# Merging two masked key blocks into one row with a predicated copy, in a hybrid decoder layer

## Chip, core and metric

The kernel runs on one core of a Trainium2 chip. The metric is device time in microseconds (us). A core has five engines that the profile names PE (TensorE, matrix multiply, with PEld for its weight loads), DVE (VectorE), ACT (ScalarE), POOL (GpSimd) and SP (SyncE, which here issues every DMA). Each runs its own queue of instructions in order and waits on semaphores for what other engines produce.

## What is computed

One decoder layer over 1024 tokens, width 1024: an input projection feeds three groups of heads (sliding-window attention, a gated linear recurrence, and a chunked delta-rule state update), and an output projection, a residual sum and a LayerNorm end it. The change is in the attention:

```
qb = q.reshape(bsz, nb, BLOCK, A_KV_HEADS, grp, HEAD_DIM) * (HEAD_DIM ** -0.5)
kb, vb = band(k), band(v)                      # previous block of 128 keys and own block: 256 keys
s = einsum("bnqhgd,bnkhd->bnhgqk", qb, kb)
diff = qi + BLOCK - kj
band_mask = (diff >= 0) & (diff < WINDOW)      # BLOCK = WINDOW = 128
s = where(mask, s, -inf)
m = maximum(max(s, axis=-1), sink)
p = exp(s - m)
denom = sum(p, axis=-1) + exp(sink - m)
o = einsum("bnhgqk,bnkhd->bnqhgd", p / denom, vb)
```

Query i of a block may see key j of the previous block only if j > i, and key j of its own block only if j <= i. So each of the 128 positions j belongs to exactly one of the two blocks, and each query sees exactly 128 keys (in the first block of the sequence only those of its own block).

## The kernel before

The sequence is worked in two halves (h = 0, 1) of 512 tokens. Every projection is a set of matmuls with 512 columns, three for each product of 128 rows, because weights and inputs are split into a high and a low part (`wh_`/`wl_`, `xh`/`xl`). Their results stand in PSUM tiles `pj_...` (`pj_q0` to `pj_q3` the queries of two heads each, `pj_ak` and `pj_av` the keys and values, `pj_ga`, `pj_gb`, `pj_gc` the gates, `pj_k`, `pj_r`, `pj_v` the state group's inputs). ACT makes the high parts of the weights, POOL or DVE the low ones, by two lists of names. PSUM has eight banks in three rings: three for `pj`, two for the state group (`rw`), three (`g`) that the attention's `sp`, `tp`, `pv` share with the recurrence's `lg`.

Attention has 32 blocks, named h_g_n: half, pair of heads, block of 128 queries. `evac_q` copies a projected query tile out of PSUM (ACT the high part, DVE the low one). `scores_stream` then runs for each block: four matmuls into `sp` (2 heads x 256 keys); on DVE one custom reduction for each head that masks, scales, writes the negated scores to SBUF `s` and leaves the row's bound in `mn`; on ACT an exponential of 257 columns for each head (the sink is column 256, put there by POOL) that also sums the row; a reciprocal on DVE; on POOL the sum of the two halves of 128 columns; and on DVE one scaling for each head. `turn_stream` transposes the row on PE into `tp`; DVE multiplies it by a triangle `pmask` for the previous block's part of `PT`, ACT or DVE copies `tp`, and POOL subtracts to get the own block's part. `pv_stream` multiplies `PT` by the values. Four of the 32 blocks (n = 0 of h = 0) have no previous block, and take 128 columns.

Around it run the state group and the recurrence. The state group's scores `sc` lead over DRAM to a triangular inverse, which DVE does in 31 steps of two instructions for each half (`it`, `TW`, after a first product `G`). `rwkv_v` puts centred values into `UV` (row sums `ms` of the transposed `vp`). `rwkv_chain` then goes through eight chunks in order for each half: PE `ch`, a copy `u0`, PE `ch` again, copies into `UV`, PE again, and the new state `S` (two DVE instructions) that is copied into `UV` for the next chunk. The output projection `o` comes last, and its first half fills PE between chunks of the second half.

What sets the order: the generators (`scores_stream`, `rwkv_stream` and so on) are merged by a string of letters (`MERGED`), which fixes the program. Then a table `ISSUED` puts every engine's instructions into another order, as numbers that index that engine's own list; dependencies between neighbours of the new order are added without a semaphore. The table comes from a planner that is not in the file. Nearly all instructions carry the line 248 in the profile, that of the helper which records them (237 in the changed kernel), so they are told apart by tiles.

Of the kernel before, what the change touches and what calls it, by code (L numbers as in the profile page):

```python
# [1338 lines left out]
```

## Time and profile before

| | before |
|---|---|
| median of 3 runs | 524.44 us |
| lowest and highest run | 524.26 and 528.27 us |
| the profiled execution, its own time | 519.97 us |
| its span in the profile | 518.2 us |
| mean granted TensorE clock | 0.985 |
| PEld, DVE, ACT, POOL busy | 365.0, 381.0, 258.1, 240.1 us |
| DMA moved | 46.30 MB, mean 89 GB/s |

The profiled execution ran 4.5 us below the median of the three runs; its span and the 1.8 us around it make up its own 519.97 us. Busy time of an engine is the union of its instructions. For PE that is nearly the whole span, so what is to be read is where PE sits idle or runs at a lower clock, who ends those waits, and what that engine had in its queue ahead of the awaited instruction. The rows follow in the prediction.

### The profile page before, as it was taken

To read this page: it belongs to the slowest core of one execution; us is meant where nothing else is said; L and a number is where in the kernel's file an instruction comes from. 1 tells how busy PE (TensorE), PEld (TensorE's weight loads), DVE (VectorE), ACT (ScalarE), POOL (GpSimd) and SP (SyncE) were. 2 spreads that over 40 slices of the span, in tenths; PEclk is the share of its full clock that TensorE was granted. 3 is DMA by queue.
4 is the path that set the end of the run, shared out by engine and by line. 5 is a ranking of instruction groups with operands and counts; after the bars stand their busy time and mean duration, and the time that the engine had idled before them with its cause. 6 is when DMAs were issued, how large, how long until landed. Compare 5 with 4: busy or idle time off the path is not lost.

```text
span 518.2 us, 8768 instructions
## 1 busy us (share of the span) xinstructions
PE 485.7 (94%) x3086; PEld 365.0 (70%) x3086; DVE 381.0 (74%) x916; ACT 258.1 (50%) x535; POOL 240.1 (46%) x285
## 2 busy tenths in 40 slices
PE   8999989979989899999998979999899899999994
PEld 6777667756766667677676858866666567878884
DVE  5966797898995478668658888888967523649984
ACT  4327737554646737475777434448746436400000
POOL 4621564144657202332567625666777606644010
PEclk9999999989999999999999999999999899999998
DMA  8900214221214432322131522311171017013531
GB/s 279 337 0 1 63 42 100 84 82 41 63 40 88 127 103 63 122 62 86 59 101 42 123 81 67 97 46 56 62 130 46 24 39 244 0 41 123 202 133 71
DMA packets 45979, 46.30 MB, mean 89 GB/s; under 512 B 25832, under 2 KB 27112, under 8 KB 45936
## 3 DMA queue, kind: packets, MB, share of 16 engines
q1 hardware_dynamic: 45936, 45.75, 29.0%
q8 instruction: 24, 0.39, 0.3%
q14 instruction: 19, 0.16, 0.1%
HBM read 39.95 MB, written 5.78 MB: 88 GB/s over the span
## 4 chain that ended last, share of the span: by engine, by line
PE 61%; DVE 23%; DMA 5%; issue 3%; ACT 3%; SPq 2%; POOL 2%; DVEq 0%; ACTq 0%; POOLq 0%
PE o L248 17%; PE c L248 5%; PE pj_ga L248 4%; DVE s L248 3%; PE pj_q L248 3%; PE ch L248 3%; PE pj_xb L248 3%; PE pj_r L248 2%; PE sp L248 2%; PE pj_gc L248 2%; SPq L248 2%; PE pj_k L248 2%; PE yp L248 2%; PE pv L248 2%; DVE TW L248 2%
## 5 line engine op out<-in xcount | busy, mean ns | idle before, releaser
L248 ACT ACTIVATE s<-s,mn 128x257 f32<-128x257 f32 (+1 forms) x64 | 31.4, 492 | 21.2 <-DVE mn L248 19.2
L248 PE MATMUL o<-wol,yh 128*128 128x512 f32 (+1 forms) x90 | 32.9, 370 | 0.0
L248 PE MATMUL o<-woh,yh 128*128 128x512 f32 (+1 forms) x90 | 32.5, 377 | 0.0
L248 PE MATMUL o<-woh,yl 128*128 128x512 f32 (+1 forms) x90 | 32.4, 373 | 0.0
L248 PE MATMUL o<-wo,yh 128*128 128x512 f32 (+1 forms) x108 | 32.1, 372 | 0.0
L248 POOL TENSOR_TENSOR s<-s 128x256 f32<-128x256 f32 x28 | 21.3, 765 | 22.6 <-ACT s L248 13.8
L248 DVE CUSTOM_DVE_ANT_0 s<-sp,con,dv 128x256 f32<-128x256 f32 (+1 forms) x64 | 27.2, 461 | 4.7 <-PE sp L248 4.4
L248 PE MATMUL pj_ga<-xh,wl_ga 128*128 128x512 f32 x64 | 26.5, 415 | 2.3 <-DVE wl_ga L248 2.3
L248 POOL TENSOR_TENSOR wl_ga<-wr_ga,wh_ga 128x512 fp32r<-128x512 f32 x14 | 19.1, 1365 | 20.2 <-ACT wh_ga L248 17.7
L248 DVE TENSOR_SCALAR s<-s,mn 128x128 f32<-128x128 f32 x64 | 26.0, 428 | 2.7 <-POOL s L248 2.7
L248 PE MATMUL pj_ga<-xh,wh_ga 128*128 128x512 f32 x64 | 26.3, 413 | 0.0
L248 PE MATMUL pj_ga<-xl,wh_ga 128*128 128x512 f32 x64 | 26.0, 406 | 0.0
L248 PE MATMUL pj_q<-xl,wh_q 128*128 128x512 f32 x64 | 25.8, 403 | 0.0
L248 POOL TENSOR_TENSOR PT<-PT 128x256 f32<-128x256 f32 x28 | 21.0, 755 | 10.3 <-ACT PT L248 9.4
L248 PE MATMUL pj_q<-xh,wh_q 128*128 128x512 f32 x64 | 25.7, 402 | 0.0
L248 PE MATMUL pj_q<-xh,wl_q 128*128 128x512 f32 x64 | 25.5, 401 | 0.0
L248 POOL TENSOR_TENSOR mv<-mv,ec 128x1 f32<-128x1 f32 x8 | 5.9, 737 | 41.7 <-DVE mv L248 41.7
L248 DVE TENSOR_TENSOR TW<-TW,it 128x126 f32<-128x126 f32 (+22 forms) x62 | 23.6, 381 | 0.8
L248 POOL TENSOR_TENSOR yl<-y,yh 128x512 fp32r<-128x512 f32 x16 | 22.0, 1393 | 3.5 <-PE o L248 1.9
L248 DVE SCALAR_TENSOR_TENSOR xres<-xres,mv,ln 128x512 f32<-128x512 f32 x32 | 23.5, 775 | 0.1
L248 PE MATMUL sp<-KH,q 128*128 128x256 f32 (+1 forms) x64 | 18.6, 314 | 5.0 <-DVE q L248 3.9
L248 PE MATMUL pv<-PT,vtok 128*64 128x128 f32 x240 | 21.4, 288 | 1.1 <-DVE PT L248 1.1
(347 smaller groups left out, 1546.1 us busy)
## 6 DMA issues: line engine op xcount, KB each, us to landing
xr<-in_xT SPq DMA_DIRECT2D x16, 256.0 KB, 3.6
wr_ga<-in_w_t SPq DMA_DIRECT2D x16, 256.0 KB, 2.6
wr_q<-in_w_t SPq DMA_DIRECT2D x16, 256.0 KB, 2.5
wor<-in_w_o SPq DMA_DIRECT2D x16, 256.0 KB, 3.1
xres<-in_x SPq DMA_DIRECT2D x8, 512.0 KB, 3.2
out<-xres SPq DMA_DIRECT2D x16, 256.0 KB, 2.0
wr_xb<-in_w_t SPq DMA_DIRECT2D x8, 256.0 KB, 2.7
wr_gb<-in_w_t SPq DMA_DIRECT2D x8, 256.0 KB, 2.6
```

Source lines behind the costliest of these rows:

```text
L248: self.ins.append(getattr(self.engine, op)(*args, **kw).ins)
```

## The change

The scale 1/8 moves from the reduction into `evac_q`. The scores stay in PSUM: a predicated copy on DVE writes the previous block's scores over the own block's columns where j > i (in the first block a constant of -1e30), so that one row of 128 remains. Column 127 of the previous part, which is no longer needed, takes the sink. A reduction over 129 columns gives the negated maximum of both heads at once, and the exponential reads those 129 columns of PSUM and writes `s`. The two halves need no sum any more. The scaling by the reciprocal moves from DVE to ACT. After the transpose, one DVE product with both triangles (`pmask` is now 256 wide) writes both parts of `PT`.

```
 def evac_q(g, h, ps):
-            A.copy(q[rs, j], ps[rs])
+            A.activation(q[rs, j], ps[rs], AF.Copy, scale=0.125)
-            V.tensor_sub(q[HS[1 - j], j], ps[rs], q[rs, j].bitcast(F32))
+            V.scalar_tensor_tensor(q[HS[1 - j], j], ps[rs], 0.125, q[rs, j].bitcast(F32),
+                                   op0=ALU.mult, op1=ALU.subtract)
...
 def scores_stream():
-                    st = wt("s", (128, 2, 257), NS, name=f"s_{h}_{g}_{n}")
+                    st = wt("s", (128, 2, 129), NS, name=f"s_{h}_{g}_{n}")
...
+                    past = neg.unsqueeze(2).broadcast_to([128, 2, 128]) if w0 else sp[:, :, 0:128]
+                    V.copy_predicated(sp[:, :, 128:256], prevm, past)
+                    V.tensor_copy(sp[:, :, 127:128], PR["sink"][:, g::4].unsqueeze(2))
+                    V.tensor_reduce(mn[:, 0:2], sp[:, :, 127:256], axis=AX.X, op=ALU.max, negate=True)
                     for j in range(2):
-                        hq = g + 4 * j
-                        P.tensor_copy(st[:, j, 256:257], nsink[:, hq:hq + 1])
-                        V.tensor_tensor_reduce(st[:, j, w0:256], sp[:, j, w0:256], C["amask"][:, w0:256],
-                                               scale=-0.125, scalar=nsink[:, hq:hq + 1], op0=ALU.add,
-                                               op1=ALU.min, accum_out=mn[:, j:j + 1])
-                        A.activation(st[:, j, w0:257], st[:, j, w0:257], AF.Exp, scale=-1.0,
-                                     bias=mn[:, j:j + 1], accum_out=mn[:, 2 + j:3 + j])
+                        A.activation(st[:, j], sp[:, j, 127:256], AF.Exp, bias=mn[:, j:j + 1],
+                                     accum_out=mn[:, 2 + j:3 + j])
                     V.reciprocal(mn[:, 2:4], mn[:, 2:4])
-                        (V if CE[n % len(CE)] else P).tensor_add(st[:, :, 128:256], st[:, :, 128:256],
-                                                                 st[:, :, 0:128])
                     for j in range(2):
-                        V.tensor_scalar_mul(st[:, j, 128:256], st[:, j, 128:256], mn[:, 2 + j:3 + j])
+                        A.activation(st[:, j, 1:129], st[:, j, 1:129], AF.Copy, scale=mn[:, 2 + j:3 + j])
...
 def turn_stream():
-                V.tensor_mul(PT[:, 0], tp, C["pmask"].unsqueeze(1).broadcast_to([128, 2, 128]))
-                    copy(f"pt{h}{g}{n}", PT[:, 1], tp)
-                    P.tensor_sub(PT[:, 1], PT[:, 1], PT[:, 0])
+                V.tensor_mul(PT, tp.unsqueeze(1).broadcast_to([128, 2, 2, 128]),
+                             C["pmask"].rearrange("p (b t) -> p b t", b=2).unsqueeze(2)
+                             .broadcast_to([128, 2, 2, 128]))
...
 ISSUED = {
 "vector": (
-    "82 84 83 80-81 48-49 0-2 5 4 3 6-8 10 9 41 38-39 50 46 51 42 40 37 76 43-44 36 45 35 47 162 52 34 53-54 56 "
...
```

PE keeps its 2461 instructions and SP its 196. DVE goes from 918 to 815, ACT from 473 to 516, POOL from 290 to 170. All five orders in `ISSUED` are new; `MERGED` and the two lists of who splits and copies what are as before. Three places matter below. A name such as `wl_ga2_0_0` is the low part of one half of the weights of gate tile ga2 in the first half of the sequence.

First, DVE in the first half of the sequence, around the split `wl_ga2` and the query split `q0`. Before, in the middle of the inverse:

```order
L248 TENSOR_TENSOR it_0_5_834<-G_0_708,TW_0_711 128x78
L248 SCALAR_TENSOR_TENSOR y_0_4_965<-tr_0_0_949,G_gb0_0_923 128x512
L248 TENSOR_TENSOR TW_0_711<-TW_0_711,it_0_5_834 128x26x3
L248 COPY hlast_461<-tr_0_0_949 128x1
L248 TENSOR_TENSOR it_0_6_855<-G_0_708,TW_0_711 128x100
L248 COPY xb_1_0_1067<-xbc_460 128x3
L248 TENSOR_TENSOR TW_0_711<-TW_0_711,it_0_6_855 128x25x4
L248 COPY xbc_460<-xb_1_0_1067 128x3
L248 TENSOR_TENSOR it_0_7_858<-G_0_708,TW_0_711 128x96
L248 TENSOR_TENSOR wl_ga2_0_0_1151<-wr_ga2_0_0_1071,wh_ga2_0_0_1150 128x512
L248 TENSOR_TENSOR TW_0_711<-TW_0_711,it_0_7_858 128x24x4
```

The same engine and place in the changed kernel, ahead of the inverse's first step:

```order
L237 TENSOR_REDUCE ms_0_0_763<-vp_0_0_758 128x8
L237 TENSOR_TENSOR wl_ga2_0_0_1151<-wr_ga2_0_0_1071,wh_ga2_0_0_1150 128x512
L237 SCALAR_TENSOR_TENSOR UV_0_757<-ms_0_0_763,vp_0_0_758 64x4x64
L237 TENSOR_REDUCE ms_0_1_774<-vp_0_1_769 128x8
L237 SCALAR_TENSOR_TENSOR UV_0_757<-ms_0_0_763,vp_0_0_758 64x4x64 x3
L237 SCALAR_TENSOR_TENSOR UV_0_757<-ms_0_1_774,vp_0_1_769 64x4x64 x4
L237 SCALAR_TENSOR_TENSOR q0_0_1172<-pj_q0_0_1129,q0_0_1172 64x512
L237 TENSOR_TENSOR G_0_708<-G_0_708,dd_0_534 128x1024
L237 SCALAR_TENSOR_TENSOR q0_0_1172<-pj_q0_0_1129,q0_0_1172 64x512
L237 SCALAR_TENSOR_TENSOR G_ga0_0_1120<-G_ga0_0_1120,pj_ga0_0_1077 128x512
L237 TENSOR_TENSOR it_0_0_716<-G_0_708,TW_0_711 128x31
```

The split `wl_ga2` stood behind seven steps of the inverse and half of the eighth, and now stands ahead of all of them; the query split stands around the product `G`, where it used to follow the ninth step.

Second, PE in the second half, at the first scores `sp_1_0_0`. Before:

```order
L248 MATMUL vp_1_0_3057<-con_63,xs_v0_1_2801 128x128 x4
L248 MATMUL pj_gb1_1_3389<-xh_1_1_2343,wl_gb1_1_0_3306 128x512
L248 MATMUL pj_gb1_1_3389<-xh_1_2_2354,wh_gb1_1_0_3305 128x512
L248 MATMUL vp_1_1_3068<-con_63,xs_v1_1_2842 128x128 x2
L248 MATMUL pj_gb1_1_3389<-xl_1_2_2355,wh_gb1_1_0_3305 128x512
L248 MATMUL pj_gb1_1_3389<-xh_1_2_2354,wl_gb1_1_0_3306 128x512
L248 MATMUL pj_xb1_1_3577<-xh_1_0_2339,wh_xb1_1_0_3546 128x512
L248 MATMUL sp_1_0_0_3340<-KH_465,q0_1_3321 128x256
```

In the changed kernel:

```order
L237 MATMUL pj_q0_1_3232<-xh_1_7_2394,wl_q0_1_1_3223 128x512
L237 MATMUL pj_ga1_1_3676<-xh_1_0_2287,wl_ga1_1_0_3617 128x512
L237 MATMUL pj_ga1_1_3676<-xh_1_1_2291,wh_ga1_1_0_3616 128x512
L237 MATMUL pj_ga1_1_3676<-xl_1_1_2292,wh_ga1_1_0_3616 128x512
L237 MATMUL pj_ga1_1_3676<-xh_1_1_2291,wl_ga1_1_0_3617 128x512
L237 MATMUL pj_ga1_1_3676<-xh_1_2_2302,wh_ga1_1_0_3616 128x512
L237 MATMUL pj_ga1_1_3676<-xl_1_2_2303,wh_ga1_1_0_3616 128x512
L237 MATMUL pj_ga1_1_3676<-xh_1_2_2302,wl_ga1_1_0_3617 128x512
L237 MATMUL pj_ga1_1_3676<-xh_1_3_2327,wh_ga1_1_0_3616 128x512
L237 MATMUL pj_ga1_1_3676<-xl_1_3_2328,wh_ga1_1_0_3616 128x512
L237 MATMUL sp_1_0_0_3288<-KH_465,q0_1_3269 128x256
```

The scores moved behind the projections xb1, ga0 and part of ga1: between the last `sc` of the half and `sp_1_0_0` the PE queue held 48 matmuls of 512 columns, and now holds 91. On DVE the split of `q0_1`, which these scores wait for, stood behind six steps of the inverse and now stands behind nine.

Third, DVE in the chain of the second half, from the state of chunk 1 to its copy into `UV`. Before:

```order
L248 TENSOR_TENSOR PT_1_3_2_4430<-tp_1_3_2_4427,con_63 128x256
L248 TENSOR_TENSOR S_1_1_4120<-ch_1_1_3963,S_1_0_3938 128x128
L248 TENSOR_TENSOR S_1_1_4120<-S_1_1_4120,wc_1_2557 128x128
L248 TENSOR_SCALAR s_1_3_3_4232<-s_1_3_3_4232,mn_1_3_3_4233 128x128
L248 COPY UV_1_3056<-S_1_1_4120 64x2x64
```

In the changed kernel:

```order
L237 TENSOR_TENSOR PT_1_2_3_4004<-tp_1_2_3_4001,con_63 128x512
L237 TENSOR_TENSOR S_1_1_4020<-ch_1_1_3879,S_1_0_3854 128x128
L237 TENSOR_REDUCE mn_1_3_0_4075<-sp_1_3_0_4076 128x2
L237 TENSOR_TENSOR S_1_1_4020<-S_1_1_4020,wc_1_2505 128x128
L237 COPY UV_1_3004<-S_1_1_4020 64x2x64
L237 COPY_PREDICATED sp_1_3_1_4091<-con_63,sp_1_3_1_4091 128x2x128
L237 COPY sp_1_3_1_4091<-par_64 128x2
```

The scaling of a late attention block that stood between the state and its copy is gone from this engine; a reduction of an earlier block stands between the two instructions of the state instead. On PE the last matmul of `sp_1_3_3`, the last scores of all, stood inside chunk 0 of this chain and now stands behind chunk 3.

More of the change, by code (lines that the diff above doesn't have):

```diff
@@ L48 @@
 X0 = (1, 0, 0, 0, 0, 0, 0, 0)
-CE = (0,)
-ME = (0,)
 OL = (0,)
@@ L220 @@
 for _name, _w in (("ident", 128),
-                  ("smask", 128), ("amask", 256), ("pmask", 128)):
+                  ("smask", 128), ("prev", 128), ("pmask", 256)):
     CON[_name] = slice(_n, _n + _w)
@@ L400, in hybrid_kernel @@
     fs, fb = (dcol(2), dcol(2)), (dcol(2), dcol(2))
-    bab, nsink = dcol(4), dcol(8)
+    bab, neg = dcol(4), dcol(1)
     sp4, nsp4 = dcol(2), dcol(2)
@@ L413, in hybrid_kernel @@
     V.tensor_scalar_mul(bab, PR["bab"], 0.5)
-    V.tensor_scalar_mul(nsink, PR["sink"], -1.0)
+    V.memset(neg, NEG)
     sc = s(pers, "sc", [128, 16], 1)
@@ L920, in evac_q @@
         for j, rs in enumerate(HS):
-            A.copy(q[rs, j], ps[rs])
+            A.activation(q[rs, j], ps[rs], AF.Copy, scale=0.125)
         for j, rs in enumerate(HS):
-            V.tensor_sub(q[HS[1 - j], j], ps[rs], q[rs, j].bitcast(F32))
+            V.scalar_tensor_tensor(q[HS[1 - j], j], ps[rs], 0.125, q[rs, j].bitcast(F32),
+                                   op0=ALU.mult, op1=ALU.subtract)
         Q[g] = q
     PV, AQ, BQ = {}, [], []
+    prevm = C["prev"].bitcast(mybir.dt.uint32).unsqueeze(1).broadcast_to([128, 2, 128])
     def scores_stream():
@@ L942, in scores_stream @@
                         TE.matmul(sp[:, j, w0:256], q[:, j, qs], KL[:, j, ks], start=False, stop=True)
+                    past = neg.unsqueeze(2).broadcast_to([128, 2, 128]) if w0 else sp[:, :, 0:128]
+                    V.copy_predicated(sp[:, :, 128:256], prevm, past)
+                    V.tensor_copy(sp[:, :, 127:128], PR["sink"][:, g::4].unsqueeze(2))
+                    V.tensor_reduce(mn[:, 0:2], sp[:, :, 127:256], axis=AX.X, op=ALU.max, negate=True)
                     for j in range(2):
-                        hq = g + 4 * j
-                        P.tensor_copy(st[:, j, 256:257], nsink[:, hq:hq + 1])
-                        V.tensor_tensor_reduce(st[:, j, w0:256], sp[:, j, w0:256], C["amask"][:, w0:256],
-                                               scale=-0.125, scalar=nsink[:, hq:hq + 1], op0=ALU.add,
-                                               op1=ALU.min, accum_out=mn[:, j:j + 1])
-                        A.activation(st[:, j, w0:257], st[:, j, w0:257], AF.Exp, scale=-1.0,
-                                     bias=mn[:, j:j + 1], accum_out=mn[:, 2 + j:3 + j])
+                        A.activation(st[:, j], sp[:, j, 127:256], AF.Exp, bias=mn[:, j:j + 1],
+                                     accum_out=mn[:, 2 + j:3 + j])
                     V.reciprocal(mn[:, 2:4], mn[:, 2:4])
-                    if not w0:
-                        (V if CE[n % len(CE)] else P).tensor_add(st[:, :, 128:256], st[:, :, 128:256],
-                                                                 st[:, :, 0:128])
                     for j in range(2):
-                        V.tensor_scalar_mul(st[:, j, 128:256], st[:, j, 128:256], mn[:, 2 + j:3 + j])
+                        A.activation(st[:, j, 1:129], st[:, j, 1:129], AF.Copy, scale=mn[:, 2 + j:3 + j])
                     AQ.append((h, g, n, st, w0 // 128))
@@ L968, in turn_stream @@
             for j in range(2):
-                TE.transpose(tp[:, j], st[:, j, 128:256], ident)
+                TE.transpose(tp[:, j], st[:, j, 1:129], ident)
             PT = wt("PT", (128, 2, 2, 128), 4, name=f"PT_{h}_{g}_{n}")
@@ L973, in turn_stream @@
             else:
-                V.tensor_mul(PT[:, 0], tp, C["pmask"].unsqueeze(1).broadcast_to([128, 2, 128]))
-                if ME[n % len(ME)]:
-                    V.tensor_sub(PT[:, 1], tp, PT[:, 0])
-                else:
-                    copy(f"pt{h}{g}{n}", PT[:, 1], tp)
-                    P.tensor_sub(PT[:, 1], PT[:, 1], PT[:, 0])
+                V.tensor_mul(PT, tp.unsqueeze(1).broadcast_to([128, 2, 2, 128]),
+                             C["pmask"].rearrange("p (b t) -> p b t", b=2).unsqueeze(2)
+                             .broadcast_to([128, 2, 2, 128]))
             BQ.append((h, g, n, PT, b0))
@@ L1278, in _constants @@
     c["smask"] = np.concatenate([sI < t, sI <= t], 1).astype(f)
-    diff = i[:, None] + 128 - np.arange(256)[None, :]
-    c["amask"] = np.where((diff >= 0) & (diff < 128), 0.0, NEG).astype(f)
-    c["pmask"] = (i[:, None] > i[None, :]).astype(f)
+    c["prev"] = (i[:, None] < i[None, :]).astype(f)
+    c["pmask"] = np.concatenate([i[:, None] > i[None, :], i[:, None] <= i[None, :]], 1).astype(f)
     return c
```

220 rows, old and new, of the table ISSUED are left out of this document.

## The prediction

> **What bounds the kernel now.** I read the page's busy times first, then the span cut into stages, then what PE waited for, then narrow windows behind the longest waits, and last the groups of the instructions that the change touches.
>
> ```profile
> span 518.2 us, 8768 instructions
> ...
> PE 485.7 (94%) x3086; PEld 365.0 (70%) x3086; DVE 381.0 (74%) x916; ACT 258.1 (50%) x535; POOL 240.1 (46%) x285
> ...
> 100.00:160.00 60.00, 54.56 (x291) 39.64 (x290) 54.65 (x180) 32.86 (x87) 30.73 (x50) 0.97 0.19 58
> 300.00:400.00 100.00, 92.05 (x648) 68.21 (x646) 84.58 (x238) 57.26 (x137) 62.18 (x83) 0.98 0.27 72
> 60.00:100.00 40.00, 37.34 (x204) 28.59 (x203) 33.09 (x63) 21.78 (x36) 20.70 (x21) 1.00 0.25 67
> 160.00:300.00 140.00, 135.40 (x1001) 99.88 (x1001) 95.65 (x191) 89.97 (x167) 60.16 (x63) 1.00 0.33 91
> 400.00:430.00 30.00, 27.95 (x319) 19.30 (x318) 12.13 (x31) 12.30 (x36) 10.86 (x10) 0.94 0.14 46
> ```
>
> The columns after a window and its length are the busy time of PE, PEld, DVE, ACT and POOL, then the clock. PE is the bound, and the change takes no matmul away. So at most PE's idle time can go, and what a lower clock costs. Between 60 and 430 us PE idles 5.4 + 8.0 + 2.7 + 4.6 + 2.1 = 22.8 us. In the two stretches with attention (100 to 160, 300 to 400) DVE is 91% and 85% busy, so DVE sets the pace there wherever PE waits:
>
> ```profile
> PE sp L248 <- DVE q L248: 3.9, 2, 3.2
> PE tp L248 <- DVE s L248: 1.7, 4, 0.7
> PE tp L248 <- DVE mn L248: 1.4, 1, 1.4
> PE pv L248 <- DVE PT L248: 1.1, 1, 1.1
> ...
> 106.30 0.50 PE L248 MATMUL pj_ga<-xh,wl_ga 128*128 128x512 f32 x1 [2.31 <-DVE wl_ga L248]
> 307.75 0.50 PE L248 MATMUL sp<-KH,q 128*128 128x256 f32 x2 [3.23 <-DVE q L248]
> 405.80 0.45 PE L248 MATMUL ch<-UV,X 128*64 128x64 f32 x6 [1.82 <-DVE UV L248]
> ...
> 107.20:110.60 3.40, 3.23 (x8) 1.99 (x6) 3.37 (x4) 1.60 (x3) 2.81 (x2) 0.54 0.55 154
> 308.60:312.00 3.40, 3.40 (x13) 2.88 (x13) 3.15 (x10) 0.62 (x1) 0.00 (x0) 0.54 0.00 0
> 407.60:411.00 3.40, 3.40 (x25) 2.31 (x24) 1.23 (x4) 1.90 (x6) 1.41 (x2) 0.54 0.00 0
> ```
>
> The first rows are sums of waits (total, times, longest), the next ones the three longest waits where they ended, and the last ones windows again. The three are for `wl_ga` (2.3 us, up to 106.3), `q` (3.2, up to 307.75) and `UV` (1.8, up to 405.8). A little behind each lies a stretch of 3.4 us in which the clock was 0.54, so that it lost 0.46 x 3.4 = 1.6 us of matmul work.
>
> **The change on each engine.** These groups carry the prices:
>
> ```profile
> L248 DVE CUSTOM_DVE_ANT_0 s<-sp,con,dv 128x256 f32<-128x256 f32 (+1 forms) x64 | 27.2, 461 | 4.7 <-PE sp L248 4.4 <-PE tp L248 0.2
> L248 DVE TENSOR_SCALAR s<-s,mn 128x128 f32<-128x128 f32 x64 | 26.0, 428 | 2.7 <-POOL s L248 2.7
> L248 DVE DVE_READ_ACCUMULATOR2_ANT mn<- 128x1 f32 x64 | 5.2, 81 | 0.0
> L248 DVE TENSOR_TENSOR PT<-tp,con 128x256 f32<-128x256 f32 x28 | 11.6, 420 | 3.9 <-PE tp L248 3.5
> L248 DVE TENSOR_TENSOR X<-sc,con 128x256 f32<-128x256 f32 x16 | 6.3, 414 | 1.5 <-PE sc L248 1.3
> L248 DVE RECIPROCAL mn<-mn 128x2 f32<-128x2 f32 x32 | 5.0, 160 | 4.9 <-ACT s L248 4.5
> L248 DVE TENSOR_REDUCE ms<-vp 128x8 f32<-128x512 f32 x4 | 2.6, 682 | 0.0
> L248 DVE TENSOR_TENSOR y<-bo,xs_v 128x512 f32<-128x512 f32 x4 | 2.7, 684 | 0.8 <-PE bo L248 0.8
> L248 DVE TENSOR_TENSOR q<-pj_q,q 64x512 fp32r<-64x512 f32 x16 | 11.0, 688 | 4.0 <-ACT q L248 3.7
> ...
> L248 ACT ACTIVATE s<-s,mn 128x257 f32<-128x257 f32 (+1 forms) x64 | 31.4, 492 | 21.2 <-DVE mn L248 19.2 <-POOL PT L248 1.4
> L248 ACT ACTIVATE s<-s,mn 128x129 f32<-128x129 f32 x8 | 3.2, 401 | 4.1 <-DVE mn L248 4.1
> L248 ACT COPY UV<-S 64x128 f32<-64x128 f32 x15 | 4.5, 299 | 6.3 <-DVE S L248 6.2
> L248 ACT COPY PT<-tp 128x256 f32<-128x256 f32 x24 | 8.9, 371 | 19.3 <-DVE PT L248 19.1
> L248 ACT CAST q<-pj_q 64x512 fp32r<-64x512 f32 x16 | 9.2, 578 | 3.2 <-PE pj_q L248 3.0
> ...
> L248 POOL TENSOR_TENSOR s<-s 128x256 f32<-128x256 f32 x28 | 21.3, 765 | 22.6 <-ACT s L248 13.8 <-DVE s L248 6.4 <-PE pj_q L248 1.6
> L248 POOL TENSOR_TENSOR PT<-PT 128x256 f32<-128x256 f32 x28 | 21.0, 755 | 10.3 <-ACT PT L248 9.4 <-DVE PT L248 0.7
> L248 POOL COPY s<-dv 128x1 f32<-128x1 f32 x64 | 12.7, 234 | 17.3 <-PE tp L248 12.0 <-DVE TW L248 1.7 <-issue 1.3
> ```
>
> DVE loses 27.2 + 26.0 + 5.2 + 11.6 = 70.0 us. It gets 32 predicated copies of 256 elements, which the trace doesn't show. The nearest row is the masked product `X` out of PSUM with 256 elements, 0.414 us; I take that. The upper bound is 0.684, the `y` row with 512 elements, if the copy passes twice over its data; the lower bound 0.34, half of the `ms` reduction. The 32 sink copies of two elements go by the reciprocal's 0.16 (5.1 us), the 32 reductions of 258 elements by 0.414 too (13.2; bounds 0.34 and 0.682), and the 28 products of 512 by 0.684 (19.2). That is 13.2 + 5.1 + 13.2 + 19.2 = 50.7 us, so DVE falls by 19 us of 381, with the bounds by 2 to 24.
>
> ACT loses 31.4 us of exponentials and 21 of 24 `PT` copies (7.8). It gets 64 exponentials of 129 columns at 0.401 (25.7) and 64 scalings of 128 columns, between 0.299 and 0.401, say 0.35 (22.4). It rises by 9 us of 258 and stays half idle, so I count nothing for it on the path; if ACT ran late, `tp` would wait for it. POOL loses 21.3 + 21.0 + 12.7 = 55.0 us of 240. The scale in `evac_q` keeps count and shape (`q`, 0.578 on ACT and 0.688 on DVE), so it costs nothing. SP issues the same DMAs in nearly the same order; the weights' buffers that it waits for are freed by splits, none of which gets later by a lighter POOL.
>
> None of this lies on PE. It counts only where PE waits, and there the new order counts as much as the durations.
>
> **The sum, wait by wait.**
>
> (a) `wl_ga`, 2.3 us, and the shorter wait for `q` close behind it, 3.9 - 3.2 = 0.7 us. Nothing of attention stood ahead of them on DVE: the inverse did. The new order puts the low part of ga2 and the query split ahead of the inverse. The wait and its clock loss go: 2.3 + 0.7 + 1.6 = 4.6 us. The inverse starts later for it, by two instructions of 0.69 us; it is late next.
>
> (b) `q`, 3.2 us. DVE was still among the inverse and the `ms` sums when PE arrived at `sp_1_0_0`. Now 91 matmuls of 512 columns instead of 48 lie between the last `sc` and these scores. How far apart two of them start, and what a step of the inverse costs:
>
> ```profile
> 116.02 0.39 PE L248 MATMUL pj_ga<-xl,wh_ga 128*128 128x512 f32 x1
> 116.25 0.40 PE L248 MATMUL pj_ga<-xh,wl_ga 128*128 128x512 f32 x1
> ...
> L248 DVE TENSOR_TENSOR TW<-TW,it 128x126 f32<-128x126 f32 (+22 forms) x62 | 23.6, 381 | 0.8
> ```
>
> The 43 more at 0.23 us give DVE 10 us more until PE arrives. Three more steps of the inverse ahead of the split, each with one such `TW` product of 0.38 us and an `it` product of about the same size, take 2.3 us of that back, and gate and convolution steps there a few more. 3.2 + 1.6 = 4.8 us go.
>
> (c) `UV`, 1.8 us. Here attention is to blame itself:
>
> ```profile
> 403.19 1.34 DVE L248 TENSOR_SCALAR s<-s,mn 128x128 f32<-128x128 f32 x1
> 404.56 1.19 DVE L248 COPY UV<-S 64x128 f32<-64x128 f32 x1
> ...
> 403.16 2.50 POOL L248 TENSOR_TENSOR yl<-y,yh 128x512 fp32r<-128x512 f32 x2
> ```
>
> A scaling that takes 0.43 us on average took 1.34 beside a POOL subtraction that began just ahead of it, and the copy that the chain waited for came behind it. The scaling is gone from DVE, so 1.8 + 1.6 = 3.4 us go. The copy itself can still meet a POOL subtraction.
>
> (d) The waits of `tp` and `pv` for attention's own steps, 1.7 + 1.4 + 1.1 = 4.2 us. The chain of a block loses the sum on POOL (0.765) and the subtraction (0.755) and gets shorter scalings, but the new order also leaves less room between `sp` and `tp`. I count half, 2.1 us.
>
> (e) New waits. The query split needs ACT 2 x 0.578 and one more DVE step of 0.688, 1.8 us and the semaphores, and the new order leaves 8 matmuls (1.9 us) ahead of `sp_0_0_0` where it left 12: I count three such places at 0.4 us. The rest of the old idle time, 22.8 - 3.9 - 2.3 - 1.8 - 4.2 = 10.6 us, came from waits that the old order did not foresee; a new order will have such ones as well, and at new places a third more: 3.6 us. Together 4.8 us.
>
> 4.6 + 4.8 + 3.4 + 2.1 - 4.8 = 10.1 us. The profiled execution took 519.97 us with its span of 518.2, so the next like it would take 510. The median of the runs was 524.44, 4.5 us more, and against that I forecast 514.4 us.
>
> [...]
>
> **The rivals.**
>
> The clock losses stay. Three stretches of 3.4 us at half clock may come from many short waits around them, not from the long one: the third wait, 1.8 us, was the shortest. Then 3 x 1.6 of the gain stays away: 524.4 - 5.3 = 519.1, just on the edge of 1%, so that half of its chance goes to either side. Chance 0.12. [...]
>
> The waits move. DVE remains the engine that PE waits for, at 80% or so in the same stretches, and a tighter order meets it elsewhere; (a) to (d) come back in full. 524 us, chance 0.18.
>
> Scores hold their bank longer. A bank of `sp` was free after two reductions and two accumulator reads, 2 x (0.461 + 0.081) = 1.1 us. Now it waits for copy, sink and reduction on DVE and both exponentials on ACT, 0.41 + 0.16 + 0.41 + 2 x 0.40 = 1.8 us, and `g` has three banks for `sp`, `tp` and `pv`, for which PE waits in order. Against it: the order was made for three banks. If all 32 blocks show the extra 0.7 us, 22 us come on top of a gain of 14.9 without (e): 524.4 - 14.9 + 22.4 = 532 us. It decides from 0.62 us per block, (14.9 + 5) / 32, where the kernel gets slower than by 1%. Chance 0.12.
>
> More goes than the named waits. If the lighter POOL also takes away DVE delays like the one in (c), there are no new waits (e) and a quarter of the other 10.6 us goes: 514.4 - 4.8 - 2.6 = 507 us. Chance 0.16.
>
> **Chances and range.** The forecast has 0.42, the rivals 0.58. About 1% (5.2 us) is what a measurement of this kernel tells from no change. Faster by more than that: 0.42 + 0.16 + 0.06 = 0.64; within: 0.06 + 0.18 = 0.24; slower: 0.12. The range of 505 to 526 us holds all but the slow case and some of each end. DVE's bounds, 2 to 24 us less, lie in it: at 2 us, (d) and the quarter of the other waits fall away, which stays below 520.
>
> **What would show it.** Right: no wait of PE over 2 us between 60 and 430 us, at most one stretch at half clock there, PE idle of some 14 us in place of 22.8; predicated copies near 0.41 us; ACT near 267, DVE near 362, POOL near 185 us busy. (a) and (b) are wrong if `pj_ga` or `sp` still wait over 1 us for `wl_ga` or `q`; (c) if `ch` waits for `UV` over 1 us. Waits of `sp` matmuls for ACT's `s` would speak for the bank; `tp` that waits for ACT, for a late ACT. The forecast is wrong altogether if PE's idle time is the same and only its releasers have new names.

## The result and the profile after

| | before | after |
|---|---|---|
| median of the runs, us | 524.35 | 501.81 |
| lowest to highest, us | 518.60 to 528.27 | 499.51 to 503.27 |
| profiled execution, us | 519.97 | 500.65 |

The ratio is 0.9601 with the 95% interval 0.9509 to 0.9694; measured again it was 0.9558 [0.9512, 0.9605]. The change takes 4% off, more than twice the forecast, and 501.81 lies below the range's low end of 505. The profiled executions differ by 19.3 us. A few executions took over 1.5% longer than the fastest of their kernel, most of them at a clock of 0.962 to 0.975; the medians here and below include them, the ratios leave them out.

The page of the changed kernel, its span and busy times:

```profile
span 498.9 us, 8538 instructions
...
PE 473.1 (95%) x3086; PEld 363.3 (73%) x3086; DVE 360.4 (72%) x813; ACT 260.6 (52%) x578; POOL 180.6 (36%) x165
```

The windows of the prediction, of the changed kernel (busy time of PE, PEld, DVE, ACT and POOL, then the clock):

```profile
60.00:100.00 40.00, 37.22 (x202) 28.91 (x202) 30.92 (x54) 23.41 (x39) 21.02 (x22) 0.96 0.26 77
100.00:160.00 60.00, 55.10 (x310) 42.59 (x309) 53.26 (x155) 35.05 (x104) 16.76 (x13) 0.97 0.23 63
160.00:300.00 140.00, 136.41 (x1015) 101.40 (x1015) 95.20 (x178) 90.66 (x176) 50.16 (x46) 1.00 0.28 87
300.00:400.00 100.00, 96.62 (x845) 73.58 (x843) 80.36 (x209) 65.37 (x181) 38.16 (x30) 1.00 0.28 78
400.00:430.00 30.00, 29.45 (x180) 22.31 (x180) 10.34 (x14) 14.11 (x27) 16.29 (x14) 1.00 0.34 115
```

PE's idle time there is 2.8 + 4.9 + 3.6 + 3.4 + 0.6 = 15.3 us, where it was 22.8. But the surprise is in the first fence: PE is busy for 473.1 us, where it was 485.7, with the same 3086 matmul rows. Of the 19.3 us, 6.7 came out of PE's idle time in the whole span (32.5 to 25.8) and 12.6 out of time that counts as busy. Between 300 and 400 us PE starts 845 rows instead of 648, since the second half's attention and chain are through earlier.

How much earlier the work gets there shows in the matmuls `gp`, with which the chain of each half begins: first the rows of their tile before, then after (count, shortest, median and longest in ns, start of the first and of the last).

```profile
L248 PE MATMUL gp<-T,X x128: 191/191/212, 171.0 to 388.5; 32*32 32x32 f32 x128
```

```profile
L237 PE MATMUL gp<-T,X x128: 191/191/212, 164.3 to 360.2; 32*32 32x32 f32 x128
```

The first half's chain begins 6.7 us earlier, the last `gp` of the second half 28.3 us earlier. Part of that is only another order, since dense matmuls were moved behind the chain; 19.3 us are left at the end.

What PE waited for in the changed kernel, longest sums first:

```profile
PE pj_ga L237 <- DVE q L237: 2.7, 2, 2.1
PE sp L237 <- DVE q L237: 1.9, 2, 1.2
PE lg L237 <- DVE lxh L237: 1.8, 1, 1.8
...
PE sc L237 <- DVE M L237: 1.5, 1, 1.5
...
PE tp L237 <- ACT s L237: 1.1, 2, 0.9
```

The waits for `wl_ga`, for `q` at `sp_1_0_0` and for `UV` are gone, `tp` and `pv` wait 1.1 us instead of 4.2, and no `sp` waits for ACT's `s`. New is `pj_ga`, which waits for `q`.

### The profile page after: what moved, and what is told of

Same layout as the page of the kernel before. It is cut to its first block, busy times and chain, and to the rows that moved or that the text cites. A ratio compares the mean times of both kernels' runs of the same rounds, so it can differ in the third digit from the quotient of the medians.

```text
span 498.9 us, 8538 instructions
## 1 busy us (share of the span) xinstructions
PE 473.1 (95%) x3086; PEld 363.3 (73%) x3086; DVE 360.4 (72%) x813; ACT 260.6 (52%) x578; POOL 180.6 (36%) x165
## 4 chain that ended last, share of the span: by engine, by line
PE 71%; DVE 17%; DMA 3%; issue 3%; ACT 2%; POOL 2%; SPq 1%; DVEq 0%; POOLq 0%; ACTq 0%
PE o L237 18%; PE pj_q L237 5%; PE pj_ga L237 5%; PE c L237 5%; PE pj_gc L237 4%; PE ch L237 3%; PE pj_xb L237 3%; PE sp L237 3%; PE pj_gb L237 3%; PE pv L237 2%; PE pj_v L237 2%; PE pj_av L237 2%; PE pj_r L237 2%; PE yp L237 2%; PE sc L237 2%
## 5 line engine op out<-in xcount | busy, mean ns | idle before, releaser
L237 ACT ACTIVATE s<-sp,mn 128x129 f32<-128x129 f32 x64 | 22.9, 365 | 18.4 <-DVE mn L237 10.2
L237 POOL TENSOR_TENSOR yl<-y,yh 128x512 fp32r<-128x512 f32 x16 | 20.8, 1318 | 21.3 <-ACT yh L237 13.3
L237 POOL TENSOR_TENSOR wl_q<-wr_q,wh_q 128x512 fp32r<-128x512 f32 x13 | 16.9, 1301 | 29.3 <-ACT wh_q L237 29.3
L237 PE MATMUL pj_q<-xh,wh_q 128*128 128x512 f32 x64 | 25.8, 403 | 0.0
L237 DVE TENSOR_TENSOR PT<-tp,con 128x512 f32<-128x512 f32 x28 | 19.2, 687 | 5.0 <-PE tp L237 4.6
L237 ACT ACTIVATE s<-s,mn 128x128 f32<-128x128 f32 x64 | 21.9, 396 | 1.7 <-DVE mn L237 1.3
L237 PEld LDWEIGHTS o<-wo,yh 128*128 128x128 f32 x108 | 19.4, 188 | 3.7
L237 DVE SCALAR_TENSOR_TENSOR xres<-xres,mv,ln 128x512 f32<-128x512 f32 x32 | 22.1, 745 | 0.0
L237 DVE SCALAR_TENSOR_TENSOR xres<-xres,o 128x512 f32<-128x512 f32 (+1 forms) x18 | 11.0, 621 | 15.0 <-PE o L237 14.0
L237 DVE TENSOR_TENSOR TW<-TW,it 128x126 f32<-128x126 f32 (+22 forms) x62 | 21.1, 340 | 0.9
L237 PE MATMUL o<-wo,yl 128*128 128x512 f32 (+1 forms) x54 | 20.1, 371 | 0.0
```

What stands on the lines that cost most here:

```text
L237: self.ins.append(getattr(self.engine, op)(*args, **kw).ins)
```

## The experiments

| run | what | median, us | ratio to before, 95% interval |
|---|---|---|---|
| e1_new_ops_old_order | changed operations, old order | 530.56 | 1.0139 [1.0060, 1.0218] |
| e1b_new_ops_old_order_DVE_scale | the same, scalings on DVE | 533.27 | 1.0209 [1.0129, 1.0289] |
| e2_old_ops_new_order | old operations, new order, one DVE instruction misplaced at the start | 541.94 | 1.0335 [1.0271, 1.0400] |
| e2b_old_ops_new_order | the same without the misplaced instruction | 534.14 | 1.0260 [1.0179, 1.0340] |
| e3_scale_on_DVE | changed kernel, scalings back on DVE | 508.93 | 0.9727 [0.9668, 0.9787] |
| e4_POOL_load_back | changed kernel, POOL's load back | 514.33 | 0.9804 [0.9737, 0.9872] |
| e5_POOL_memsets | the same load, only writing | 505.51 | 0.9719 [0.9661, 0.9777] |
| e6_PT_split_back | changed kernel, PT split as before | 510.80 | 0.9833 [0.9768, 0.9899] |
| h1_q_ahead_of_G | changed kernel, one exchange on DVE | 500.25 | 0.9551 [0.9504, 0.9597] |
| h2_narrow_pred_copy | changed kernel, narrow predicated copy | 497.54 | 0.9530 [0.9467, 0.9594] |
| f1_before_narrow_POOL | kernel before, narrow sums on POOL | 517.34 | 0.9895 [0.9853, 0.9936] |
| f2_before_narrow_scaling | kernel before, narrow scalings | 515.78 | 0.9874 [0.9777, 0.9972] |
| g1_splits_and_copy_moved | kernel before, steps (a) and (c) alone | 521.70 | 0.9976 [0.9934, 1.0018] |
| a2_after_again | changed kernel again | 500.66 | 0.9558 [0.9512, 0.9605] |

The median of the kernel before differs by 3 us from one series of runs to another, so a difference between two of these kernels is given by the medians and, where it matters, by the ratios.

### The operations alone, and the order alone

The first run keeps the changed operations and takes all old orders; what has no old place stands where its time was in the trace of before.

```diff
 ISSUED = {
 "tensor": (
-    "0-2 6 3-4 9 5 15 10-11 21-22 7-8 16-17 23-24 12 26 13-14 32 18-20 33 27 25 35-36 38 28 34 41 29-31 37 43 42 "
+    "0-4 18-20 5 12 6 15-17 7-8 26 23-24 38-40 35-37 9 13-14 10-11 21 27 32-34 29-31 22 28 41-42 25 187-189 "
...
```

> The changed operations in the order of the kernel before: PE and SP word for word the old order, the predicated copy where the first reduction stood, sink and reduction where the second stood, the exponentials right behind it, the scalings on ACT at the time when the old ones ran on DVE. Theory Work (the lighter DVE and POOL are what counts, in any order): most of the 22 us, 503 to 510 us, PE busy falls by 8 us or more, and the waits for wl_ga and for q at sp_1_0_0 get shorter. Theory Order (the new sequence is what counts): 518 to 527 us, these waits stay at 2 to 3 us, PE busy stays within 4 us of 485.7. Theory Both (an order is worth what it is only with the durations for which it was planned): 512 to 524 us, PE idle about as before. My guess is Both.

530.56 us: slower than before by 1.4%, though DVE had 13.5 us less to do (367.5) and POOL 54, and above the ranges of all three theories. The second run is its mirror image.

> The operations of the kernel before in the new order: PE and SP word for word the new order, the two old reductions where predicated copy and row reduction stand, the old scalings on DVE at the time when the new ones run on ACT, the sums and subtractions on POOL at the time when their inputs are there. Theory Order: 501 to 509 us. Theory Work: 518 to 528 us. Theory Both: 512 to 528 us, with tp and pv waiting for DVE and POOL for 8 us or more in sum, since the new order leaves less room between sp and tp than 0.77 + 0.76 us of POOL and 2 x 0.43 us of DVE need.

541.94 us, again above all three ranges, but one misplaced DVE instruction at the start kept PE waiting for 6.8 us; without it:

> The earlier run with the old operations in the new order, with one DVE instruction of the start put right (the sink's sign ran as the third and waited for its parameters, which held the first xh up by 6.8 us). 532 to 537 us if that alone was the matter. Order: still 509 or less; Both: above 518.

534.14 us. So each part alone makes the kernel slower, by 1.4 and 2.6%, and both together make it faster by 4%. The waits say why. What PE waited for in the first run:

```profile
PE tp L239 <- ACT s L239: 3.5, 5, 2.0
PE sp L239 <- ACT s L239: 3.0, 4, 0.9
```

And with the old operations in the new order:

```profile
PE tp L245 <- DVE s L245: 12.5, 12, 2.6
PE pv L245 <- POOL PT L245: 4.4, 6, 1.6
```

The new order leaves too little room for the old chain through DVE and POOL. In the old one `sp` waits for exponentials, which now read its bank: this is the rival of the bank. Whether the first run suffered from scalings that come late on ACT instead was told apart by putting them on DVE at their old places:

```diff
-                        A.activation(st[:, j, 1:129], st[:, j, 1:129], AF.Copy, scale=mn[:, 2 + j:3 + j])
+                        V.tensor_scalar_mul(st[:, j, 1:129], st[:, j, 1:129], mn[:, 2 + j:3 + j])
```

> The changed operations in the old order as in the first run, but with the scalings on DVE, word for word at their old places. If the first run lost its time to scalings that came late on ACT (tp waits for ACT s, 3.5 us): 518 to 524 us. If it lost it to scores that hold their bank longer (sp waits for ACT s, 3.0 us; the exponentials now read the bank): the waits of sp stay and it takes 528 to 536 us, DVE's 64 scalings on top.

533.27 us, and the wait of `sp` is the same to the tenth:

```profile
PE sp L240 <- ACT s L240: 3.0, 4, 0.8
...
PE tp L240 <- ACT s L240: 2.8, 2, 2.2
```

Late scalings are not it. `tp` still waits for ACT's `s`, which ACT writes here only in the exponentials; `tp` shares its banks with `sp`, so this points to the bank as well, 5.8 us in sum. How much of the loss hangs on the bank stays open: the lower clock of the profiled execution (0.975 in the first run against 0.985) doesn't explain the ratio, since the executions of the kernel before in the same series had clocks of 0.966 to 0.988 and those of the first run 0.968 to 0.987.

### One part undone in the changed kernel

The scalings back on DVE, by the same diff, in the new order:

> The changed kernel with one part undone: the 64 scalings go from ACT back to DVE, at the same times. DVE gains 64 x 0.25 to 0.43 = 16 to 27 us, ACT loses 22. Work: DVE's load is what PE waits for, so time rises by 6 us or more (508 to 515). Order: within 2 us of the changed kernel (500 to 504). The rows of tp would then wait for DVE s instead of ACT s.

508.93 us, 7.1 us more than the changed kernel (1.3 to 1.8% by the ratios), as expected if PE waits for DVE's load. DVE has 375.7 us to do, and `tp` waits 6.0 us for DVE's `s`, where it waited 1.1 for ACT's.

POOL's load back, with no one waiting for its results:

```diff
                     V.reciprocal(mn[:, 2:4], mn[:, 2:4])
+                    if not w0:
+                        P.tensor_add(scr, con[:, 0:256], con[:, 256:512])
...
                              .broadcast_to([128, 2, 2, 128]))
+                P.tensor_sub(scr, con[:, 0:256], con[:, 256:512])
```

> The changed kernel with 28 sums and 28 subtractions of 128x256 put back on POOL, on constants and into a scratch tile that nobody reads, near the times of the old ones: POOL gains 42 us or so, and no data wait is added. If POOL's load slows DVE by itself (they get in each other's way at memory), DVE's TW and s rows get longer by 5% or more and the time rises by 3 us or more (505 to 510). If only dependencies on POOL's results counted, the time stays within 2 us (500 to 504).

514.33 us, above the 505 to 510 expected: POOL work that nobody reads costs 12.5 us by the medians, 10.6 to 13 by the ratios (0.9804 against 0.9601 and 0.9558). The same load as writes alone:

```diff
-                        P.tensor_add(scr, con[:, 0:256], con[:, 256:512])
+                        P.memset(scr, 0.0)
...
-                P.tensor_sub(scr, con[:, 0:256], con[:, 256:512])
+                P.memset(scr, 0.0)
```

> As the run with POOL's load put back, but its 56 operations only write: zeros over 768 columns, some 0.75 us each by the row of a 512-column one (0.53). POOL gains the same 42 us at the same places in its order. If it is POOL's reading beside DVE's two-input operations on SBUF that slows DVE, most of the 12.5 us goes away: 501 to 506 us, TW back near 340 ns; the plain copies UV<-S may stay slow. If POOL's own lateness is the cause (its splits come later), the time is again 512 to 516 us.

505.51 us: 3.7 us more than the changed kernel by the medians, 6 to 8 by the ratios. The groups of five DVE operations tell what happens, first in the changed kernel (busy us, mean ns behind the bar):

```profile
L237 DVE TENSOR_TENSOR TW<-TW,it 128x126 f32<-128x126 f32 (+22 forms) x62 | 21.1, 340 | 0.9
L237 DVE TENSOR_TENSOR it<-G,TW 128x126 f32<-128x126 f32 (+22 forms) x62 | 18.6, 300 | 0.9
L237 DVE TENSOR_TENSOR X<-sc,con 128x256 f32<-128x256 f32 x16 | 6.6, 417 | 5.8 <-PE sc L237 5.6
L237 DVE COPY UV<-ch 64x128 f32<-64x128 f32 x16 | 4.6, 288 | 3.3 <-PE ch L237 3.0
L237 DVE COPY UV<-S 64x128 f32<-64x128 f32 x15 | 4.2, 277 | 3.0 <-PE bt L237 2.5
```

With sums and subtractions back on POOL:

```profile
L239 POOL TENSOR_TENSOR scr<-con 128x256 f32<-128x256 f32 x56 | 43.3, 773 | 2.7
L239 DVE TENSOR_TENSOR TW<-TW,it 128x126 f32<-128x126 f32 (+22 forms) x62 | 26.1, 421 | 0.9
L239 DVE TENSOR_TENSOR it<-G,TW 128x126 f32<-128x126 f32 (+22 forms) x62 | 23.3, 376 | 0.9
L239 DVE TENSOR_TENSOR X<-sc,con 128x256 f32<-128x256 f32 x16 | 6.6, 418 | 7.2 <-PE sc L239 7.1
L239 DVE COPY UV<-S 64x128 f32<-64x128 f32 x15 | 6.5, 436 | 3.0 <-PE bt L239 2.5
L239 DVE COPY UV<-ch 64x128 f32<-64x128 f32 x16 | 4.6, 288 | 2.9 <-PE ch L239 2.5
```

With the memsets:

```profile
L239 POOL MEMSET scr<- 128x768 f32 x56 | 41.4, 740 | 2.0
L239 DVE TENSOR_TENSOR it<-G,TW 128x126 f32<-128x126 f32 (+22 forms) x62 | 19.2, 310 | 0.9
L239 DVE COPY UV<-S 64x128 f32<-64x128 f32 x15 | 6.0, 398 | 3.0 <-PE bt L239 2.6
```

POOL is as busy in both (43.3 and 41.4 us). The two groups with an operand in PSUM take the same to the nanosecond: `X` 417, 418 with the sums and 418 with the memsets, `UV<-ch` 288 in all three. The two with both inputs in SBUF get a quarter longer with the sums (`TW` 340 to 421 ns, `it` 300 to 376), and `it` hardly with the memsets (310). The plain copy from SBUF to SBUF (`UV<-S`) gets longer with both (277 to 436 and 398). So POOL's load slowed DVE by itself here. The sums, which read SBUF, cost between 4.5 us (by the ratios) and 8.8 (by the medians) more than the memsets, which only write. The rest stays with the memsets; whether it comes from the copies that took longer or from POOL's own later splits was not told apart.

PT split again, with its real dependencies:

```diff
-                V.tensor_mul(PT, tp.unsqueeze(1).broadcast_to([128, 2, 2, 128]),
-                             C["pmask"].rearrange("p (b t) -> p b t", b=2).unsqueeze(2)
-                             .broadcast_to([128, 2, 2, 128]))
+                V.tensor_mul(PT[:, 0], tp, C["pmask"][:, 0:128].unsqueeze(1).broadcast_to([128, 2, 128]))
+                copy(f"pt{h}{g}{n}", PT[:, 1], tp)
+                P.tensor_sub(PT[:, 1], PT[:, 1], PT[:, 0])
```

> The changed kernel with one part undone: PT again as a product of 256 on DVE, a copy (ACT or DVE as before) and a subtraction on POOL, at the times of the one product. DVE loses 28 x 0.27 = 7.5 us, gains 7 copies, ACT gains 8, POOL 21 us with data waits. If DVE's busy sum were what counts: 498 to 502 us. If POOL beside DVE and the longer chain to pv count: 506 to 512 us with pv waiting for POOL PT.

510.80 us with DVE's busy time unchanged (360.2). The longer way to `pv` has its own price, and its wait is the longest sum on PE:

```profile
PE pv L241 <- POOL PT L241: 4.0, 9, 1.1
```

The three costs can't be added: this run's 28 subtractions are half of the load put back on POOL above, and every undone part runs in an order that was made without it.

### DVE and POOL relieved in the old order, and DVE once more in the new one

In the kernel before, without any change of order:

```diff
-                        (V if CE[n % len(CE)] else P).tensor_add(st[:, :, 128:256], st[:, :, 128:256],
-                                                                 st[:, :, 0:128])
+                        (V if CE[n % len(CE)] else P).tensor_add(st[:, :, 128:129], st[:, :, 128:129],
+                                                                 st[:, :, 0:1])
...
-                    P.tensor_sub(PT[:, 1], PT[:, 1], PT[:, 0])
+                    P.tensor_sub(PT[:, 1, :, 0:1], PT[:, 1, :, 0:1], PT[:, 0, :, 0:1])
```

> The kernel before, its order untouched, with the sum of the key blocks and the subtraction for PT on one column only instead of 128 (the rest of both is left out): POOL loses some 35 us and the chain of a block gets shorter by 2 x 0.6 us; DVE, ACT and PE are as before. Lock (POOL beside DVE costs by itself, in any order): 510 to 517 us. Order: POOL's work was planned for, so 520 to 525 us.

517.34 us, 1.05% faster, just above the 510 to 517 us expected if POOL beside DVE costs by itself. DVE runs the same 916 instructions in 367.7 us instead of 381.0; its scalings fell from 428 ns to 328 with nothing changed but POOL's work. The other side of the same pair:

```diff
-                        V.tensor_scalar_mul(st[:, j, 128:256], st[:, j, 128:256], mn[:, 2 + j:3 + j])
+                        V.tensor_scalar_mul(st[:, j, 128:129], st[:, j, 128:129], mn[:, 2 + j:3 + j])
```

> The kernel before, its order untouched, with the 64 scalings on DVE on one column instead of 128 (the rest is left out): DVE loses 64 x (0.43 - 0.1) = 21 us, stalls beside POOL among it; POOL, ACT and PE stay. DVE sets the pace: 508 to 515 us. PE's waits that name a scaling (tp for s 1.7, UV 1.8 us) are all: 519 to 523.

515.78 us, 1.3% faster; DVE 370.9 us. And in the changed kernel:

```diff
-                    V.copy_predicated(sp[:, :, 128:256], prevm, past)
+                    V.copy_predicated(sp[:, :, 128:129], prevm[:, :, 0:1], past[:, :, 0:1])
```

> The changed kernel with the predicated copy on one column per head instead of 128 (the rest of the merge is left out): DVE loses 28 x (0.42 - 0.1) + 4 x 0.6 = some 11 us, all inside the attention stretches; PE, ACT, POOL and the order stay. If DVE's time in these stretches sets the pace: 493 to 497 us, of which most comes from the stretches between 110 and 160 and between 320 and 400 us. If PE's named waits are all that can go: within 2 us of the changed kernel (499 to 503), since none of its longest waits is for this copy.

497.54 us, between the two expected ranges and nearer to the first. The intervals overlap with those of the changed kernel; the span of the profiled execution was 494.9 against 498.9 and 498.3, with DVE at 353.6. In the profiled executions of these three runs the span fell by about half of what DVE saved: 4.0 us for 6.8 (some 2.5 of the 4.0 by a higher mean clock, 0.994 against 0.989), and in the old order 5.7 for 10.1 and 5.7 for 13.3. In the old order it came out of PE's idle time, which fell from 32.5 to 26.1 us in both runs, while PE's busy time stayed (485.7 before, 486.4 in both). In the changed kernel the list of PE's longest waits is the same with the narrow copy as without (`pj_ga` 2.6, `sp` 1.8, `lg` 1.8 us).

### Named waits removed by themselves

In the kernel before, steps (a) and (c) of the prediction and nothing else; rows of DVE as they stand now:

```diff
+TENSOR_TENSOR wl_ga2<-wr_ga2,wh_ga2
 SCALAR_TENSOR_TENSOR ti<-ti,xc
...
-TENSOR_TENSOR wl_ga2<-wr_ga2,wh_ga2
...
+TENSOR_TENSOR q0<-pj_q0,q0 x2
 SCALAR_TENSOR_TENSOR xc<-xb,par,xc
...
-TENSOR_TENSOR q0<-pj_q0,q0 x2
...
+COPY UV<-S_1_1
 TENSOR_SCALAR s_1_3_3
-COPY UV<-S_1_1
```

> The kernel before with the two moves of steps (a) and (c) alone, on DVE: the split wl_ga ahead of the step of the inverse at 101.9 us and the query split 1.4 us earlier; and the copy of the state into UV ahead of the scaling that took 1.34 us. By the prediction's sum the waits and their stretches at half clock go: 4.6 + 3.4 = 8.0 us. If DVE's lateness is only handed on (the inverse and the scores take the waits over): 0 to 2 us. If a copy on SBUF is held up by POOL's subtraction as the scaling was, (c) brings 1.3 us at most, and the copy shows over 1 us again: then 3 to 6 us in sum.

521.70 us, 0.24% with an interval across zero. The wait for `wl_ga` is gone; the next rows of PE and DVE in the timeline show who has it now:

```profile
109.98 0.62 PE L248 MATMUL sp<-KH,q 128*128 128x128 f32 x3 [2.49 <-DVE q L248]
```

```profile
107.87 1.34 DVE L248 TENSOR_TENSOR it<-G,TW 128x115 f32<-128x115 f32 x1
109.25 1.41 DVE L248 TENSOR_TENSOR q<-pj_q,q 64x512 fp32r<-64x512 f32 x2
```

The scores start 1.1 us earlier than before (111.05) and wait 2.49 us for `q` instead of 0.62, behind a step of the inverse that takes 1.34 us beside a POOL subtraction (`wl_ga`, 1.32 us from 107.76). In step (c) `ch` waits 0.6 us for `UV` instead of 1.8; the copies `UV<-S` take 382 ns on average, where they took 316. The same was tried in the changed kernel on its longest wait, for the second half of `q0` behind `G`:

```diff
 SCALAR_TENSOR_TENSOR q0<-pj_q0,q0
+SCALAR_TENSOR_TENSOR q0<-pj_q0,q0
 TENSOR_TENSOR G<-G,dd
-SCALAR_TENSOR_TENSOR q0<-pj_q0,q0
```

> The changed kernel with one exchange on DVE: the second half of the first query split ahead of the product G (128x1024, 2.15 us in the trace) instead of behind it. PE waited 2.08 us for that split, and a stretch of 3.4 us at half clock began 1.1 us later. If the clock falls behind such a wait: both go, 2.1 + 1.6 = 3.7 us less than the changed kernel, and no stretch at half clock near 108 us. If the clock falls for another reason: 2.1 us less at most, and the stretch stays. If the wait only moves (G is later by 0.7 us, and the inverse with it): less than 1 us.

The yardstick on the same chip:

> The changed kernel itself, as the measure for the next run on the same chip: 500 to 503 us.

500.25 against 500.66 us, no difference. The wait of 2.1 us went, and with it the low clock near 108 us: it was 0.53 from 107.9 to 111.3 us in the repetition, and is 1.00 here from 108.4 to 111.8. But `tp` waits longer for `s`, 2.8 us where it was 1.1:

```profile
PE tp L237 <- ACT s L237: 2.8, 3, 1.7
```

The clock fell in another place instead:

```profile
164.60:168.00 3.40, 3.40 (x10) 2.23 (x10) 0.70 (x1) 3.34 (x6) 0.00 (x0) 0.53 0.07 23
```

The wait moved to `tp`, whose longest is now 1.7 us instead of 0.9, and the loss of clock to the 3.4 us from 164.6, where the repetition has 1.00; the time stayed.

## Why the prediction was too slow

**What bounds.** The step that failed is the first: "PE is the bound, and the change takes no matmul away. So at most PE's idle time can go, and what a lower clock costs." Only 6.7 of the 19.3 us were idle time. By an estimate from the mean clock, 0.985 of 518.2 us and 0.989 of 498.9, the loss to half clock fell from 7.8 to 5.5 us, 2.3 us (windows inside the low stretches show 0.50, as from 107.5 to 110.0 us before). The other 10.3 us came out of PE's busy time, which holds parts of waits. These rows of PE from the run with steps (a) and (c) alone show one:

```profile
103.29 0.39 PE L248 MATMUL pj_q<-xl,wh_q 128*128 128x512 f32 x1
103.52 0.40 PE L248 MATMUL pj_q<-xh,wl_q 128*128 128x512 f32 x1
104.44 0.50 PE L248 MATMUL pj_ga<-xh,wh_ga 128*128 128x512 f32 x1 [0.52 <-ACT xb L248]
```

The first two matmuls of 512 columns are recorded with 0.39 and 0.40 us, and start 0.23 us apart. The third starts 0.92 us after the second and so is 0.69 us late, of which 0.52 is listed as idle. By these figures up to 0.17 us of a wait behind such a matmul counts as busy, and a wait shorter than that does not appear at all. The start times of all matmul rows show which distances got shorter. Three kinds of neighbours are a 512-column matmul followed by a 128-column one (`tp`, `pv` and others; 64 pairs before, 59 after) or by a 256-column one (`sp`; 14 and 15), and two of 64 columns in a row (the chain; 568 and 572). From start to start they took 29.6, 8.6 and 25.2 us before, and 22.5, 3.8 and 20.5 after: 16.6 of the 19.3 us, the listed waits and half clock among it. The other kinds nearly cancel out; a 128-column matmul followed by a 512-column one took 2.2 us more. Without distances over 0.6 us the first kind still fell from 0.31 to 0.29 us a pair and the last from 41 to 35 ns.

To which part of the change this belongs can be read from the runs with only one of the two. First the new operations in the old order, then the old operations in the new order:

```profile
span 530.3 us, 8549 instructions
...
PE 492.7 (93%) x3086; PEld 369.0 (70%) x3086; DVE 367.5 (69%) x813; ACT 261.4 (49%) x578; POOL 186.3 (35%) x165
```

```profile
span 533.4 us, 8786 instructions
...
PE 488.7 (92%) x3086; PEld 370.1 (69%) x3086; DVE 383.6 (72%) x916; ACT 257.5 (48%) x535; POOL 231.4 (43%) x285
```

Their mean clocks are 0.975 and 0.965. An estimate of what half clock costs is the span times the share by which the mean clock falls short of 1:

| operations, order | PE busy, us | lost to half clock | busy without it | PE idle |
|---|---|---|---|---|
| old, old (before) | 485.7 | 7.8 | 477.9 | 32.5 |
| new, old | 492.7 | 13.3 | 479.4 | 37.6 |
| old, new | 488.7 | 18.7 | 470.0 | 44.7 |
| new, new (changed) | 473.1 | 5.5 | 467.6 | 25.8 |

By the same working the two runs in the old order with less work for POOL or DVE have 477.7 and 478.2 us in the third column, and seven more runs in the new order (the repetition and those on the changed kernel) 466 to 471. So the 10 us in busy time come with the new order, whatever the operations. For the operations alone the prediction's rule nearly holds: in the new order they took PE's idle time from 44.7 to 25.8 us and the loss to half clock from 18.7 to 5.5. What in the order brings the matmuls closer together was not tried.

**DVE and POOL priced at nothing.** "None of this lies on PE. It counts only where PE waits, and there the new order counts as much as the durations" was right about where it counts. What was too small is the price of those waits. The durations themselves were right, those on ACT within 13%. In the changed kernel:

```profile
L237 ACT ACTIVATE s<-sp,mn 128x129 f32<-128x129 f32 x64 | 22.9, 365 | 18.4 <-DVE mn L237 10.2 <-PE pj_gb L237 3.4 <-DVE sp L237 2.3
L237 ACT ACTIVATE s<-s,mn 128x128 f32<-128x128 f32 x64 | 21.9, 396 | 1.7 <-DVE mn L237 1.3
...
L237 DVE TENSOR_TENSOR PT<-tp,con 128x512 f32<-128x512 f32 x28 | 19.2, 687 | 5.0 <-PE tp L237 4.6
L237 DVE TENSOR_REDUCE mn<-sp 128x2 f32<-128x258 f32 x32 | 13.1, 418 | 0.2
L237 DVE COPY_PREDICATED sp<-con,sp 128x256 f32<-128x256 uint32 x28 | 11.8, 424 | 5.9 <-PE sp L237 5.7
L237 DVE COPY sp<-par 128x2 f32<-128x2 f32 x32 | 5.0, 159 | 0.6
```

Predicted were, in us, 0.414 for the predicated copy (0.424), 0.414 for the reduction (0.418), 0.16 for the sink (0.159) and 0.684 for the product (0.687); on ACT 0.401 for the exponential (0.365) and 0.35 for the scaling (0.396). DVE came out at 360.4 us (362 predicted), ACT at 260.6 (267), POOL at 180.6 (185). What was missing is how much of PE's waiting in the new order hangs on DVE's time and on POOL's load. POOL's load, priced at nothing outside step (c), cost 11 to 13 us when it came back, and the scalings on DVE 7. In the profiled execution with the load back PE's idle time rose from 25.8 to 34.3 us and the loss to half clock from 5.5 to 10.3: 13.3 of the 15.0 us between the two spans. The prediction had seen a scaling of 1.34 us beside a POOL subtraction, took it for one place, step (c), and left the general case to a rival with 0.16.

**Steps (a) to (c).** The waits went as forecast: `wl_ga`, `q` at `sp_1_0_0`, `UV`. Their price was wrong all the same. (a) and (c) alone brought some 1.3 us by the ratio (its interval is -0.9 to 3.5 us) of the 8.0 put down for them, and by its own sign (a) is wrong, as `pj_ga` and `sp` still wait 2.1 and 1.2 us for `q`. With DVE 91% busy in that stretch, the work put ahead made the next piece late: `sp` then waited 2.49 us for `q` instead of 0.62. That is the rival "the waits move", right for the order taken by itself. (b) was not tried alone.

**Steps (d) and (e).** `tp` and `pv` wait 1.1 us instead of 4.2, better than half. The idle time left, 15.3 us, is near the 14 forecast. Since the single prices of (a) and (c) were wrong and new waits came elsewhere, that their sum fits is in part luck.

**The clock.** At most one stretch at half clock was forecast between 60 and 430 us; the profiled execution had two (0.56 from 81.0 to 84.4 us, 0.54 from 108.4 to 111.8), the repetition one (0.53 from 107.9 to 111.3). Neither this nor the rival in which the losses stay decides anything: between these two kernels it is a matter of 2 us.

**The bank.** No `sp` waited for ACT's `s` in the changed kernel, and four did in the old order with the changed operations, 3.0 us in sum. Whether the 1.1 us of `tp` in the changed kernel are for a scaling or for a bank isn't shown. The remark that the order was made for three banks held, for the new order alone.

**More goes.** This rival had half of the mechanism, a lighter POOL that takes delays away from DVE (381.0 to 367.7 us of DVE's busy time in the kernel before with narrow POOL operations). Its 507 us were too high because it too was held under PE's idle time.

Neither the operations nor the order brings any of the gain alone: the order's 10 us in busy time are lost again to waits when the old operations run in it. What stays open is which neighbours in the order matter.

## What to carry to other kernels

PE was 94% busy before, and that was no floor for the time: its busy time contained parts of waits and fell from 485.7 to 473.1 us with the same matmuls. So compare the distance from start to start with the shortest one of the same shape before setting a limit, and expect a new order to change it. DVE work taken out here, where DVE was 80 to 91% busy in the attention's stretches, was worth about half its time (4.0 us of span for 6.8, 5.7 for 10.1). Price POOL work by what it adds to DVE's rows beside it, also where nobody waits for POOL: 56 sums and subtractions that nobody read lengthened `TW` from 340 to 421 ns here and cost 10.6 to 13 us. An order and the durations that it was made for were one thing here: the operations alone were 1.4% slower than before, the order alone 2.6%, and where one piece was moved, the wait turned up behind the next (`sp` for `q`, 2.49 us; `tp` for `s`, 2.8).
